# One run of value products per unit: joining a unit's near keys with the last far keys of the unit before

## The chip, the cores and the metric

The kernel runs on one core of a Trainium2 chip. A core has a matrix engine (PE, whose weight loads are shown apart as PEld), a vector engine (DVE), a scalar engine (ACT), a general engine (POOL) and a queue of transfers (SP). PE reads its operands from SBUF and writes to PSUM, eight banks of 2 KB per partition; DVE and ACT copy from PSUM to SBUF. The metric is the device time of one execution in microseconds (us); lower is better.

## The reference

A decoder trunk of two layers over 1024 tokens with 1024 features. Only the attention of the first layer (A) is touched. It has 16 heads in 4 key groups of 4 heads, head width 64, and adds three branches, each with a sigmoid gate of its own:

```python
o = g[..., 0:1] * o_cmp + g[..., 1:2] * o_sel + g[..., 2:3] * o_win
```

`o_cmp` attends to 63 compressed key blocks, `o_win` to a causal window of 256 tokens, and `o_sel` to the 8 selected blocks of 64 keys of each query, out of all keys up to the query. Every branch is a softmax over scores plus a position bias, times values. The kernel computes `o_sel` over all causal keys, with the blocks that are not selected masked in the scores.

## The kernel before

The attention of layer A is worked in 32 *units* (g, t): key group g (4) by tile t (8) of 128 queries, t running fastest. A unit has two kinds of keys. The *near* keys are the window's, 128-key blocks `t-2` to `t` (1 to 3 blocks), together with the compressed blocks (one more block, `pc`). The *far* keys are the blocks 0 to t of the selected branch, t + 1 blocks.

For each kind PE makes scores (`near_scores` L823, `far_scores` L910 and L911, into PSUM bank `s`), DVE adds the bias and takes the minimum (L824, L826, L912), ACT makes exponentials (L803), POOL scales them by gate and denominator (L807). The weights then stand with queries on partitions, and the value products need keys there, so each 128-key block is *turned*: PE transposes it for the four heads into one bank `pt` (L371, 4 instructions; 3 banks), DVE and ACT in turn copy it to an SBUF tile `pT` (L378; 5 tiles), and PE multiplies it by the values (L436): two matmuls per block, one for each half of the heads, whose weights are 64 columns wide and which write partitions 0 to 63 and 64 to 127 of `o`. In the trace each of these matmuls leaves two records, so that a block is four records of L436. The sum of a unit stands in one half of a single PSUM bank `o`, and the two halves are used in turn; DVE copies it out at the end (L925).

`values` (L416) does this for a list of blocks, in *parts* of at most three: the blocks of a part are turned, then multiplied in one chain, the block turned last first. A unit has one near part (up to four products, `pc` the last) and ceil((t + 1) / 3) far parts, so 1, 1, 1, 2, 2, 2, 3, 3 for t = 0 to 7, 15 per group and 60 in all.

`turn(i)` (L959) issues what belongs to turn i: near scores of unit i + 2 (steps a and b), far scores of unit i (f and g), the mask (m), compressed weights (c), far values of unit i - 1 (v) and near values of unit i (n), in the order a m f v b c n g. The framework's scheduler then orders each engine's instructions by its own estimates, within the data dependencies and the orderings that `after(...)` lays down; it pulls transposes and scores in between one another, and does not keep every part's chain in one piece. After the last unit the output projection follows; its weights `ow` are loaded by SP (L1407) as the attention's tiles come free.

Of the kernel before, what the change touches and what calls it, by code (L numbers as in the profile page):

```python
# [129 lines left out]
def trunk(ctx, tc, I, out):  # L130
    nc = tc.nc
# [84 lines left out]
    def after(prev):  # L216
        return tc.issue_after(prev.ins) if prev is not None else ExitStack()
# [38 lines left out]
    def norm_to_hT(p, xget, gains, hH, hL, t0, n, wait=None, behind=(None, None), third=None):  # L256


        xs = []
        for t in range(t0, t0 + n):  # L260
            xt = xget(t)
            xn = p.tile([128, D], F32, name="nxn", bufs=4)
            with after(behind[0]), after(behind[1]):
                rs = row_scale(p, xt, xn, t == 3)
            nc.vector.tensor_scalar(xn, xt, rs, None, op0=OP.mult)
            xs.append(xn)
        for k in range(KC):
            pt = bank("mm")
            for i in range(n):
                mm = nc.tensor.transpose(pt[:, i * 128:(i + 1) * 128], xs[i][:, k * 128:(k + 1) * 128], ident)  # L270
            tk = slice(t0 * 128, (t0 + n) * 128)
            prev = split(hH[k][:, tk], hL[k][:, tk], pt[:, :n * 128], gains[:, k:k + 1])
            turn[0] = mm
            if k == (5 if t0 == 0 else 3) and wait is not None:
                keep(*wait, mm)
            if k == 2 and third is not None:
                third(prev)
        return prev
# [88 lines left out]
    def turned(p, heads, copy, n=128):  # L367

        ps = bank("pt")
        for i, h in enumerate(heads):  # L370
            prev = nc.tensor.transpose(ps[:, i * 128:(i + 1) * 128], h, ident)  # L371
        w = len(heads) * 128
        t = p.tile([128, 512], F32, name="pT", bufs=pt_bufs[0])
        if n < 128:
            copy(t[:, :len(heads) * n].rearrange("p (h q) -> p h q", q=n),
                 ps[:, :w].rearrange("p (h q) -> p h q", q=128)[:, :, 128 - n:])
        else:
            copy(t[:, :w], ps[:, :w])  # L378
        return t, prev
# [8 lines left out]
            self.i += 1  # L388
            return self.parts[(self.i - 1) % len(self.parts)]

    copies, pt_bufs = [0], [5]

    def turn_blocks(p, Ps, vs, late=()):

# [19 lines left out]
                prev = mm  # L414
        return prev

    def values(p, po, Ps, vs, first, last, behind=None, more=None):

        nb = len(vs)
        ends = [nb * (i + 1) // -(-nb // 3) for i in range(-(-nb // 3))]
        for lo, hi in zip([0] + ends, ends):
            ts = []
            for b in range(lo, hi):
                copies[0] += 1
                t, prev = turned(p, [Ps[hp][:, e, b * 128:(b + 1) * 128] for e in range(2) for hp in range(2)],
                                 (nc.scalar.copy, nc.vector.tensor_copy)[copies[0] % 2])
                ts.append(t)
            ops = [(vs[b], vs[b], ts[b - lo][:, :256], ts[b - lo][:, 256:]) for b in reversed(range(lo, hi))]  # L430
            if more is not None and lo == 0:
                ops.append(more)
            for i, (*v, ta, tb) in enumerate(ops):
                with after(prev), after(behind if lo == i == 0 else None):
                    for e, t in enumerate((ta, tb)):
                        mm = nc.tensor.matmul(po[64 * e:64 * e + 64, :256], v[e], t, start=first and lo == i == 0,  # L436
                                              stop=last and hi == nb and i == len(ops) - 1, skip_group_check=True)
                prev = mm
        return prev

    def pipelined(jobs, lag=1):

# [26 lines left out]
    vc = ares.tile([128, G, 128], F32, name="vc")  # L469
# [4 lines left out]
    with ExitStack() as c:  # L474
# [62 lines left out]
        with ExitStack() as c2:  # L537
            np_ = pool(c2, "pn")

            def xget(t):  # L540
                xt = np_.tile([128, D], F32, name="nx", bufs=4)
                nc.sync.dma_start(xt, x_in[t * 128:(t + 1) * 128])
                return xt
# [7 lines left out]
            first = [xget(t) for t in range(2)]  # L551
# [10 lines left out]
            rows_made, behind, rows = None, (None, None), make_rows()  # L562
            for t0 in (0, 2):
                done = t0 * 128, t0 * 128 + 256
                prev = norm_to_hT(np_, lambda t: first[t], g_mix[0], *hT, t0, 2, (fill, 4 if t0 == 0 else 3, ones),
                                  behind, second if t0 == 0 else None)
                behind = prev, scaled_rest[0]
# [12 lines left out]
            prev = norm_to_hT(np_, xlate, g_mix[0], *hT, 4, 4, behind=behind)  # L580
# [58 lines left out]
        steps = compress(0, kc2, wts)  # L639
# [45 lines left out]
        def proj_q(ch):  # L685
            proj_T(wts.load(W[:, 128 * ch:128 * ch + 128], KC, 128), hT, evac_q(ch))
# [3 lines left out]
        steps = compress(1, kc2, wts)  # L690
# [41 lines left out]
        grp = {}  # L732
# [57 lines left out]
        units = [(g, t) for g in range(G) for t in range(NT)]  # L790
# [91 lines left out]
        def near_values(g, t):  # L882
            pc = blocks_[g, t][0]
            pT, _ = turned(wk, [pc[:, 2 * c:2 * c + 2, :] for c in range(2)], nc.vector.tensor_copy)
            po = po_[g, t] = outs()
            k0 = max(t - 2, 0)
            ends[0] = values(wk, po, grp["P2", g, t], [grp["V", 1, g, b // 4][:, b % 4, :] for b in range(k0, t + 1)],
                             True, False, ends[0], (vc[:, g, :64], vc[:, g, 64:], pT[:, :256], pT[:, :256]))

        def far_scores(g, t, hp):  # L890

# [28 lines left out]

        def far_values(g, t):
            po = po_[g, t]
            ends[0] = values(wk, po, grp["P1", g, t], [grp["V", 0, g, b // 4][:, b % 4, :] for b in range(t + 1)],
                             False, True)
            nc.vector.tensor_copy(oT[:, 2 * g:2 * g + 2, tok(t)], po.rearrange("p (c q) -> p c q", q=128))  # L925

        def loads(g, t):
# [22 lines left out]
        for i in (1, 2):  # L950
# [5 lines left out]
        steps = dict(a=lambda u: near_scores(*u, 0), b=lambda u: near_scores(*u, 1), c=lambda u: block_weights(*u),  # L956
                     m=lambda u: block_mask(*u), f=lambda u: far_scores(*u, 0), g=lambda u: far_scores(*u, 1),
                     n=lambda u: near_values(*u), v=lambda u: far_values(*u))
        def turn(i):  # L959
            if 0 <= i < len(units):  # L960
                loads(*units[i])
            if i >= 0:
                load_kw(i + 3)
            for what, d in [('a', 2), ('m', 0), ('f', 0), ('v', -1), ('b', 2), ('c', 2), ('n', 0), ('g', 0)]:
                if 0 <= i + d < len(units):
                    steps[what](units[i + d])
        proj_q(6)
        for i in range(-2, 0):
            turn(i)
# [6 lines left out]
    with ExitStack() as c:  # L976
        kB = pool(c, "aB")
        wk = pool(c, "aw")
# [8 lines left out]
        outs, ends = Turns([o_[:, :256], o_[:, 256:]]), [None]  # L987
# [857 lines left out]
    with ExitStack() as c:  # L1845
        wk = pool(c, "bw")
# [10 lines left out]
        grp = {}  # L1857
# [64 lines left out]
        outs, behind, held, formed = Turns([o_[:, :256], o_[:, 256:]]), [None], [], [None]  # L1922
# [208 lines left out]
```

## Time and profile before

| what | value |
|---|---|
| median of 3 runs | 2744.61 us (2741.62 to 2746.01) |
| the profiled execution | 2744.88 us, of which its span is 2743.1 |
| first and last record of a layer A value product (L436) | starts at 283.0 us and 666.0 us |
| records of L436 on PE | 576 far, 336 near, 128 compressed |
| granted TensorE clock | 0.999 |

The span is what the profiler saw of the program on the core. Where rows are quoted, the busy time of PE is that of pipelined matmuls: the durations of neighbours overlap, and what one costs is read from the start of one to the start of the next. A row of the chain of waits gives the piece of time that the chain spent in a group of instructions, a row of the timeline a start and the time to the last end, with the idle time of PE before it in brackets.

### The profile page before, as it was taken

The numbers are of one execution on the slowest core, as the hardware profiler recorded it, in microseconds if no ns is written. First come the engines' busy times: TensorE is split into PE (matmuls) and PEld (weight loads), VectorE is DVE, ScalarE is ACT, GpSimd is POOL, SyncE is SP. The second block draws the span as 40 slices with busy tenths as digits, with TensorE's granted clock in tenths as the row PEclk, the third lists the DMA queues.
The fourth block names the chain that finished last, engine by engine and source line by source line (L and its number), as shares of the span: only waits on it lengthen the run. The fifth ranks groups of instructions, "written<-read, shape, count | busy, mean of one in ns | idle before, by whom it ended". The sixth has DMA issues, their size and how long they took to land.

```text
span 2743.1 us, 42940 instructions
## 1 busy us (share of the span) xinstructions
PE 2712.7 (99%) x14448; PEld 2211.6 (81%) x14448; DVE 2208.2 (81%) x4532; ACT 1409.4 (51%) x3165; POOL 1385.5 (51%) x1446
## 2 busy tenths in 40 slices
PE   9999999999999999999999999999999999999999
PEld 8988676776888888888878788888878888888887
DVE  5443888987988889899884678688898888898888
ACT  5531776775643343343454444577766443343435
POOL 3135755552365656656446787311104755656562
PEclk9999999999999999999999999999999999999999
DMA  5578663224122222222124455697341211112112
GB/s 174 188 235 299 171 164 104 64 70 146 51 73 66 78 73 67 69 62 77 58 89 125 136 154 165 211 272 235 111 177 50 72 57 58 51 54 62 54 54 77
DMA packets 291900, 312.24 MB, mean 114 GB/s; under 512 B 50300, under 2 KB 229165, under 8 KB 291680
## 3 DMA queue, kind: packets, MB, share of 16 engines
q1 hardware_dynamic: 271280, 247.30, 30.0%
q0 software_dynamic: 20400, 62.20, 7.3%
q8 instruction: 114, 1.87, 0.3%
q14 instruction: 106, 0.87, 0.1%
HBM read 241.99 MB, written 81.04 MB: 118 GB/s over the span
## 4 chain that ended last, share of the span: by engine, by line
PE 86%; DVE 6%; DMA 3%; issue 1%; ACT 1%; POOL 1%; SPq 1%; POOLq 0%; ACTq 0%; DVEq 0%
PE ux L1244 18%; PE uy L1244 15%; PE dx L1054 8%; PE pt L371 6%; PE dr L1054 6%; PE o L436 4%; PE dr L1244 4%; PE mm L239 3%; PE mm L240 3%; PE mm L241 3%; PE o L412 2%; DVE pl L1013 2%; PE s L823 1%; PE dx L1244 1%; PE s L911 1%
## 5 line engine op out<-in xcount | busy, mean ns | idle before, releaser
L1013 DVE TENSOR_TENSOR pl<-oT,ph 128x512 fp32r<-128x512 f32 x336 | 348.7, 1057 | 72.4 <-ACT ph L1012 18.8
L1012 ACT ACTIVATE ph<-oT 128x512 fp32r<-128x512 f32 x342 | 209.7, 627 | 229.9 <-PE ux L1244 54.3
L371 PE MATMUL pt<-ident,P 128*128 128x128 f32 x1536 | 231.5, 277 | 2.9 <-ACT pT L378 1.3
L1013 DVE TENSOR_TENSOR pl<-oTb,ph 128x512 fp32r<-128x512 f32 x228 | 205.7, 926 | 25.1 <-PE dr L1054 17.3
L1012 ACT ACTIVATE ph<-oTb 128x512 fp32r<-128x512 f32 x234 | 142.6, 627 | 159.1 <-PE ux L1244 51.0
L807 POOL TENSOR_SCALAR P<-P,sm,gates 128x384 f32<-128x384 f32 (+7 forms) x256 | 183.1, 726 | 80.2 <-DVE sm L805 57.3
L371 PEld LDWEIGHTS pt<-ident,P 128*128 128x128 f32 x1536 | 174.3, 140 | 59.9 <-issue 42.6
L1449 POOL TENSOR_TENSOR oT<-oT,gffn 128x512 f32<-128x512 f32 x92 | 113.8, 1247 | 214.8 <-DMA oT<-in_ffn_w_up_dram 158.8
L1059 DVE TENSOR_TENSOR xrfx<-xrfx,dr 128x512 f32<-128x512 f32 x320 | 204.1, 679 | 12.9 <-PE dr L1054 12.9
L1059 DVE TENSOR_TENSOR xrfx<-xrfx,dx 128x512 f32<-128x512 f32 x320 | 204.4, 678 | 1.2 <-PE dx L1054 1.2
L1449 POOL TENSOR_TENSOR oTb<-oTb,gffn 128x512 f32<-128x512 f32 x92 | 115.9, 1268 | 151.9 <-DMA oTb<-in_ffn_w_up_dram 85.9
L803 ACT ACTIVATE P<-P,m 128x384 f32<-128x384 f32 (+7 forms) x256 | 170.6, 668 | 35.7 <-DVE m L916 14.1
L378 DVE COPY pT<-pt 128x512 f32<-128x512 f32 (+1 forms) x208 | 131.7, 644 | 34.9 <-PE pt L371 28.3
L1937 ACT ACTIVATE P<-P,st 128x384 f32<-128x384 f32 (+2 forms) x256 | 139.3, 546 | 24.6 <-DVE st L1932 24.3
L378 ACT COPY pT<-pt 128x512 f32<-128x512 f32 x176 | 100.4, 577 | 99.0 <-PE pt L371 98.5
L1932 DVE CUSTOM_DVE_ANT_0 P<-s,T 128x384 f32<-128x384 f32 (+2 forms) x256 | 110.2, 477 | 6.2 <-PE s L1962 1.7
L1054 PE MATMUL dx<-ph,pl 128*128 128x512 f32 x320 | 107.2, 390 | 0.4 <-DVE pl L1013 0.4
L1054 PE MATMUL dx<-ph 128*128 128x512 f32 x320 | 107.3, 389 | 0.0
L912 DVE CUSTOM_DVE_ANT_0 P<-s,T 128x128 f32<-128x128 f32 (+3 forms) x192 | 99.3, 550 | 8.3 <-PE s L911 8.1
L239 PE MATMUL mm<-hH,wh 128*128 128x512 f32 (+1 forms) x272 | 102.8, 379 | 0.0
L240 PE MATMUL mm<-hL,wh 128*128 128x512 f32 (+1 forms) x272 | 102.5, 379 | 0.0
L241 PE MATMUL mm<-hH,wl 128*128 128x512 f32 (+1 forms) x272 | 102.3, 377 | 0.0
(649 smaller groups left out, 8029.1 us busy)
## 6 DMA issues: line engine op xcount, KB each, us to landing
qB<-xrfx POOLq DMA_DIRECT2D x96, 256.0 KB, 5.1
oT<-in_ffn_w_up_dram SPq DMA_DIRECT2D x92, 256.0 KB, 2.9
oTb<-in_ffn_w_up_dram SPq DMA_DIRECT2D x92, 256.0 KB, 2.9
Q<-qB SPq DMA_DIRECT2D x40, 512.0 KB, 7.6
wd<-in_ffn_w_down_dram SPq DMA_DIRECT2D x60, 256.0 KB, 2.6
oT<-in_b_w_q_dram SPq DMA_DIRECT2D x48, 256.0 KB, 3.9
wraw<-in_a_w_in_dram SPq DMA_DIRECT2D x18, 512.0 KB, 5.5
KW<-kS SPq DMA_DIRECT2D x96, 96.0 KB, 2.7
```

Of the source, the lines that this page charges most:

```text
L239: nc.tensor.matmul(ps, lh, rh, start=first, stop=False, skip_group_check=bool(shared))
L240: nc.tensor.matmul(ps, lh, rl, start=False, stop=False, skip_group_check=bool(shared))
L241: return nc.tensor.matmul(ps, ll, rh, start=False, stop=last, skip_group_check=bool(shared))
L371: prev = nc.tensor.transpose(ps[:, i * 128:(i + 1) * 128], h, ident)
L378: copy(t[:, :w], ps[:, :w])
L807: nc.gpsimd.tensor_scalar(P[:, e, :n], P[:, e, :n], sm[:, e:e + 1], gate(e), op0=OP.mult, op1=OP.mult)
L1012: self.high = nc.scalar.activation(h, src, AF.Copy)
L1013: self.last = (eng or nc.vector).tensor_sub(l, src, f32(h))
L1054: nc.tensor.matmul(banks[t], part(a, t)[u], b[v], start=z == 0 and onX != 2, stop=z == 2, skip_group_check=True)
L1059: nc.vector.tensor_add(xs, xs, banks[t])
L1244: mm = nc.tensor.matmul(b, x[:, i * 128:(i + 1) * 128], ys[i], start=first and (z, i) == (0, 0), stop=(z, i) == (2, 3), skip_group_check=True)
L1449: nc.gpsimd.tensor_mul(v, v, gains[:, k:k + 4].unsqueeze(2).to_broadcast([128, 4, 128]))
```

## The change

`values` becomes a generator. With near keys (`first`) it turns the blocks and puts their products on a list `held`, and issues none. With far keys it issues a run of products for each part, and puts what is held behind the last part's products. `value_run` holds the loop that issued the products. In `turn(i)` the step v is split: all far parts of unit i - 1 but the last (`more` of them) are worked where v was, and the last part is turned after n, behind the near blocks of unit i. Its products and the held near products of unit i then go in one run. For the first unit, with no far keys before it, the held products go alone at the end of the turn. `pt_bufs` rises from 5 to 7; before layer B it is set to 6 as before.

```diff
-    copies, pt_bufs = [0], [5]
+    copies, pt_bufs = [0], [7]
...
-    def values(p, po, Ps, vs, first, last, behind=None, more=None):
+    held = []
+
+    def values(p, po, Ps, vs, first, behind, more=None):
...
-            for i, (*v, ta, tb) in enumerate(ops):
-                with after(prev), after(behind if lo == i == 0 else None):
-                    for e, t in enumerate((ta, tb)):
-                        mm = nc.tensor.matmul(po[64 * e:64 * e + 64, :256], v[e], t, start=first and lo == i == 0,
-                                              stop=last and hi == nb and i == len(ops) - 1, skip_group_check=True)
-                prev = mm
-        return prev
+            last = hi == nb and not first
+            ops = [(po, first and i == 0, last and i == len(ops) - 1, op) for i, op in enumerate(ops)]
+            if first:
+                held.extend(ops)
+                continue
+            behind[0] = value_run(ops + (held if last else []), prev, behind[0])
+            if last:
+                held.clear()
+            yield
+
+    def value_run(ops, *prev):
+
+        for dst, starts, stops, (*v, ta, tb) in ops:
+            with ExitStack() as c:
+                for x in prev:
+                    c.enter_context(after(x))
+                for e, t in enumerate((ta, tb)):
+                    mm = nc.tensor.matmul(dst[64 * e:64 * e + 64, :256], v[e], t, start=starts, stop=stops,
+                                          skip_group_check=True)
+            prev = mm,
+        return mm
...
-            ends[0] = values(wk, po, grp["P2", g, t], [grp["V", 1, g, b // 4][:, b % 4, :] for b in range(k0, t + 1)],
-                             True, False, ends[0], (vc[:, g, :64], vc[:, g, 64:], pT[:, :256], pT[:, :256]))
+            for _ in values(wk, po, grp["P2", g, t], [grp["V", 1, g, b // 4][:, b % 4, :] for b in range(k0, t + 1)],
+                            True, None, (vc[:, g, :64], vc[:, g, 64:], pT[:, :256], pT[:, :256])):
+                pass
...
-            ends[0] = values(wk, po, grp["P1", g, t], [grp["V", 0, g, b // 4][:, b % 4, :] for b in range(t + 1)],
-                             False, True)
+            for n, _ in enumerate(values(wk, po, grp["P1", g, t], [grp["V", 0, g, b // 4][:, b % 4, :]
+                                                                   for b in range(t + 1)], False, ends), 1):
+                if n < -(-(t + 1) // 3):
+                    yield
...
-            for what, d in [('a', 2), ('m', 0), ('f', 0), ('v', -1), ('b', 2), ('c', 2), ('n', 0), ('g', 0)]:
+            far = steps['v'](units[i - 1]) if i > 0 else iter(())
+            steps['w'] = lambda u: next(far, None)
+            more = -(-(units[i - 1][1] + 1) // 3) - 1 if i > 0 else 0
+            for what, d in [('a', 2), ('m', 0), ('f', 0)] + more * [('w', -1)] + [('b', 2), ('c', 2), ('n', 0), ('w', -1),
+                                                                                  ('g', 0)]:
                 if 0 <= i + d < len(units):
                     steps[what](units[i + d])
+            if i == 0:
+                value_run(held, None)
+                held.clear()
```

How the scheduler then places the products on PE is shown at two places. In these rows a name is the tile written, then the tiles read; `V` are far values, `VW` near values, `vc` the compressed blocks' values, `P` and `pc` weights that are turned, and the products stand in L436 before and in L452 now. A row with x2 is one block.

The first place is where a group ends and the next begins: the last far part of a group's eighth unit (`V_2907`, three blocks) and the near products of the next group's first unit (`VW_3910` and `vc`). Before, on PE, the far part stood between transposes:

```order
L371 MATMUL pt<-ident,P_3922 128x128
L371 MATMUL pt<-ident,P_4024 128x128
L436 MATMUL o<-pT,V_2907 64x256 x6
L371 MATMUL pt<-ident,P_4376 128x128
L371 MATMUL pt<-ident,P_4509 128x128
```

and the near products came 16 rows later, with that unit's own far block:

```order
L910 MATMUL s<-K_3013,Q_3501 128x256
L911 MATMUL s<-KF_3907,Q_3501 128x256
L436 MATMUL o<-pT,VW_3910 64x256 x2
L436 MATMUL o<-pT,vc 64x256 x2
L436 MATMUL o<-pT,V_3019 64x256 x2
```

Now the two stand in one run:

```order
L927 MATMUL s<-K_3013,Q_3499 128x256
L928 MATMUL s<-KF_3907,Q_3499 128x256
L452 MATMUL o<-pT,V_2907 64x256 x6
L452 MATMUL o<-pT,VW_3910 64x256 x2
L452 MATMUL o<-pT,vc 64x256 x2
L371 MATMUL pt<-ident,P_4123 128x128
L371 MATMUL pt<-ident,P_4206 128x128
```

The second place is the last pair of units on PE, the last far part of the 31st (`V1`) and the near products of the 32nd (`VW10`, `vc`); here the tiles carry their numbers. Before, the near products were a run of their own, ten transposes behind the far run; its head and tail:

```order
L371 MATMUL pt_8642<-ident_67,P23_8283 128x128
L371 MATMUL pt_8683<-ident_67,P1_8533 128x128
L371 MATMUL pt_8690<-ident_67,P1_8533 128x128
L436 MATMUL o_2882<-pT_8647,VW10_7354 64x256 x2
L436 MATMUL o_2882<-pT_8640,VW10_7354 64x256 x2
L436 MATMUL o_2882<-pT_8633,VW10_7354 64x256 x2
L436 MATMUL o_2882<-pT_8626,vc_93 64x256 x2
L371 MATMUL pt_8701<-ident_67,P1_8533 128x128
```

Now seven blocks are multiplied in one run, and the block read first (`pT_8640`) was turned only two transposes ahead of it:

```order
L371 MATMUL pt_8635<-ident_67,P1_8504 128x128
L371 MATMUL pt_8683<-ident_67,P1_8533 128x128
L371 MATMUL pt_8690<-ident_67,P1_8533 128x128
L452 MATMUL o_2882<-pT_8640,V1_7368 64x256 x2
L452 MATMUL o_2882<-pT_8633,V1_7368 64x256 x2
L452 MATMUL o_2882<-pT_8626,V1_7368 64x256 x2
L452 MATMUL o_2882<-pT_8619,VW10_7354 64x256 x2
L452 MATMUL o_2882<-pT_8612,VW10_7354 64x256 x2
L452 MATMUL o_2882<-pT_8605,VW10_7354 64x256 x2
L452 MATMUL o_2882<-pT_8598,vc_93 64x256 x2
L371 MATMUL pt_8683<-ident_67,P1_8657 128x128
```

Over the stage the order has the same 520 value matmuls and 976 transposes on PE, and the same 260 copies of turned blocks, 146 on DVE and 114 on ACT, before and now. The value matmuls stand in 107 uninterrupted runs before and in 72 now; the scores stand in 138 runs before and in 162 now. Ahead of the attention and behind it the order of every engine is the same but for names and line numbers.

## The prediction

> **What bounds the kernel now.** I read the page first, then busy time by stretch, then PE's groups, then PE's timeline. The page:
>
> ```profile
> span 2743.1 us, 42940 instructions
> PE 2712.7 (99%) x14448; PEld 2211.6 (81%) x14448; DVE 2208.2 (81%) x4532; ACT 1409.4 (51%) x3165; POOL 1385.5 (51%) x1446
> PE 86%; DVE 6%; DMA 3%; issue 1%; ACT 1%; POOL 1%; SPq 1%; POOLq 0%; ACTq 0%; DVEq 0%
> ```
>
> PE is busy all the time and holds 86% of the chain of waits, so PE time saved should shorten the span wherever no other engine is close behind. Only the attention of layer A changes. Busy time by stretch (window; PE, PEld, DVE, ACT, POOL; clock, DMA), the second and third key groups cut into units with long scores and the rest, then two 12 us slices:
>
> ```profile
> 384.00:444.00 60.00, 59.20 (x414) 43.02 (x412) 54.90 (x255) 47.00 (x155) 35.79 (x61) 1.00 0.31 90
> 444.00:480.00 36.00, 35.55 (x251) 24.20 (x250) 24.84 (x105) 23.48 (x70) 20.44 (x40) 1.00 0.58 163
> 480.00:540.00 60.00, 59.61 (x418) 43.30 (x419) 55.64 (x261) 46.61 (x151) 34.75 (x60) 1.00 0.22 65
> 540.00:576.00 36.00, 35.06 (x257) 25.49 (x256) 25.43 (x112) 24.54 (x79) 18.82 (x32) 1.00 0.41 112
> 420.00:432.00 12.00, 11.93 (x88) 8.88 (x86) 11.72 (x53) 9.10 (x28) 6.90 (x12) 1.00 0.11 33
> 612.00:624.00 12.00, 11.93 (x86) 8.81 (x86) 11.79 (x53) 9.66 (x29) 6.68 (x10) 1.00 0.00 1
> ```
>
> PE is the bound, with 189.4 of 192 us. But DVE is at 92% in the long stretches (54.90 and 55.64 of 60) and at 98% in single slices. That is where a gain could get lost. The clock is full, so it explains nothing here.
>
> What does PE do there? Its groups between 283 and 667 us (count | busy, mean ns | idle before):
>
> ```profile
> L371 PE MATMUL pt<-ident,P 128*128 128x128 f32 x908 | 137.6, 279 | 2.6 <-ACT pT L378 1.3 <-DVE pT L378 0.9
> L436 PE MATMUL o<-pT,V 128*64 128x256 f32 x576 | 79.0, 392 | 2.4 <-ACT pT L378 1.8 <-DVE pT L378 0.4
> L436 PE MATMUL o<-pT,VW 128*64 128x256 f32 x336 | 43.3, 389 | 2.3 <-ACT pT L378 1.3 <-DVE pT L378 0.7
> L436 PE MATMUL o<-pT,vc 128*64 128x256 f32 x128 | 19.2, 379 | 0.0
> ```
>
> PE waits only 2.4 + 2.3 = 4.7 us for value products' operands, so removing waits can't be worth more. The price must be sought in the runs themselves. The chain of waits cuts PE's time into pieces (start, us, what; x4 of L436 is one block):
>
> ```profile
> 633.24 0.58 PE o L436 x4
> 633.82 0.59 PE pt L371 x4
> 634.40 1.01 PE o L436 x8
> ...
> 637.59 1.45 PE o L436 x12
> ...
> 641.01 1.88 PE o L436 x16
> ...
> 645.98 1.03 PE pt L371 x8
> ...
> 377.24 1.46 PE pt L371 x12
> ```
>
> Four, 8, 12 and 16 product records take 0.58, 1.01, 1.45 and 1.88 us. That is (1.88 - 0.58) / 12 = 0.108 us a record and 0.58 - 4 x 0.108 = 0.15 us once per run, whatever its length. Transposes between two product runs show the same: 0.59, 1.03 and 1.46 us for 4, 8 and 12, so (1.46 - 0.59) / 8 = 0.109 each and 0.15 once. **Each interruption of product runs by transposes thus costs PE 0.15 + 0.15 = 0.30 us that no instruction needs**: a value matmul fills 64 of 128 columns, a transpose all, and going from one to the other and back has a price. Entering from scores costs as much as from transposes:
>
> ```profile
> 648.25 0.40 PE L910 MATMUL s<-K,Q 128*128 128x512 f32 x1
> 648.48 0.39 PE L911 MATMUL s<-K,QM 80*128 80x512 f32 x1
> 648.80 0.65 PE L436 MATMUL o<-pT,V 128*64 128x256 f32 x4
> ```
>
> Scores start 0.23 us apart, the product 0.32 after the last one: 0.09 on entry, the rest of the 0.15 at the way out. Between transposes and scores nothing is paid:
>
> ```profile
> 361.46 1.09 PE L371 MATMUL pt<-ident,P 128*128 128x128 f32 x8
> 362.31 0.48 PE L910 MATMUL s<-K,Q 128*128 128x512 f32 x1
> 362.63 0.39 PE L911 MATMUL s<-K,QM 80*128 80x512 f32 x1
> 362.86 0.40 PE L910 MATMUL s<-K,Q 128*128 128x512 f32 x1
> ```
>
> From 361.46 to 362.63 is 1.17 us: eight transposes at 0.109 (0.87), one score at the 0.23 of the next pair, and 0.07, which is about the 0.15 - 0.09 due for leaving the product run ahead of them.
>
> **The change, part by part.**
>
> *Runs of products.* As issued, 32 near and 60 far runs become 60 and one. The scheduler cuts some: in PE's order 107 uninterrupted runs become 72. I price the order, since PE executes that: 35 x 0.30 = **10.5 us less**. Bounds: if only the 0.15 inside a product run goes away, for the 31 runs that the code joins, 4.6; if all 4.7 us of waits go too, 10.5 + 4.7 = 15.2. I take 10.5, since both halves of the price show at every length of run.
>
> [...]
>
> *Scores in 162 runs for 138.* By the last fence this costs nothing.
>
> *The wait ahead of a joined run.* Its first product reads the block turned last, so it waits for that copy:
>
> ```profile
> L378 DVE COPY pT<-pt 128x512 f32<-128x512 f32 (+1 forms) x144 | 88.5, 627 | 29.5 <-PE pt L371 27.6 <-PE o L436 1.1
> L378 ACT COPY pT<-pt 128x512 f32<-128x512 f32 x114 | 64.9, 577 | 75.0 <-PE pt L371 74.8
> 659.14 1.08 PE L436 MATMUL o<-pT,V 128*64 128x256 f32 x8 [0.62 <-ACT pT L378]
> 664.85 1.52 PE L436 MATMUL o<-pT,V 128*64 128x256 f32 x12 [0.68 <-ACT pT L378]
> ```
>
> A copy takes about 0.6 us, and with nothing between the last transpose and the run PE stands 0.6 to 0.7. Queued behind the run on PE are the unit's far scores (step g), and behind those DVE's bias and minimum and ACT's exponentials. Cover counts, then: pricing the rows between the last transposes that a run needs and the run by the spacings above, 19 of 107 runs have under 0.7 us before, 16 of 72 now. Fewer, but now they are long joined runs. Bounds: in proportion to runs, 4.7 x 72 / 107 = 3.2, 1.5 us gained; if all 16 stand 0.65 and the rest as now, 10.4 against 4.7, 5.7 lost. I take nothing, nearest the 4.7 that 19 such runs cost today.
>
> *Buffers.* A joined run reads up to 3 + 4 = 7 blocks, all seven `pT`, where 5 served runs of four. The next copy waits for the run's end, but its transposes stand behind the run on PE anyway: nothing, at worst one copy's 0.6 us per unit late on an engine that waits for transposes now (27.6 and 74.8 us above). Copies are as many, with the same split.
>
> *The stage's end.* The output projection's loads are issued as the last far scores free their tiles:
>
> ```profile
> 650.42 3.20 SPq L1407 DMA_DIRECT2D ow<-in_a_w_out_dram  x7
> 666.29 0.50 PE L239 MATMUL dx<-ph 128*128 128x512 f32 x1
> ```
>
> From the last far score (648.48, above) to the projection's first matmul PE has 54 transposes and 34 value matmuls in 7 runs before, and 58 and 36 in 6 runs now: 4 x 0.109 + 2 x 2 x 0.108 - 0.30 = 0.6 us more room for the loads, which move with the stage. (A value matmul is two records.) Nothing is lost here.
>
> Sum: 10.5 us of the profiled execution's 2744.88 (span 2743.1, 1.8 outside it), 2734.4; its time is 0.3 above the median of 2744.61, so **2734**.
>
> **The rivals.**
>
> *DVE becomes the bound.* For it: 92% in the long stretches, 98% in slices. Against: DVE's own idle time is mostly waiting for PE (the 27.6 us ahead of copies), which would shrink with PE's. If the long stretches, 60 of 96 us, gained nothing, 36 / 96 x 10.5 = 3.9 us remained: 2740.7. [...]
>
> *Slower: the joined runs stand for their last copy.* 31 times a turn's products now hang on one copy, with the near products, ready long before, behind it. If each stood the full 0.68 us shown above, 21.1 us would be lost against 10.5 gained: 2755. It decides from 10.5 / 31 = 0.34 us per joined run on. Against it: in PE's order most joined runs have transposes or scores between, and before, 19 runs with as little cover cost 4.7 us with all others.
>
> *Nothing changes.* The price belonged to each block and not to the run: against it stand the four lengths above. 2744.6.
>
> **How the numbers follow.** Forecast 0.77, DVE 0.15, slower 0.05, nothing 0.03. The forecast's own range is 2730 (nearly the 15.2) to 2738; the DVE rival pulls the upper end to 2740.5. What a measurement here can tell from no change is about 0.2%, 5.5 us: faster means below 2739.1. Most of the forecast lies there, the DVE rival just outside: faster 0.78, same 0.17, slower 0.05.
>
> **What would show it.** Right: value products on PE in 72 runs with the same 0.108 and 0.15; the stretch from first to last product about 10.5 shorter than its 383; waits ahead of products near 4.7 us. DVE rival: PE idle before scores, released by DVE's minimum, and DVE over 95% in the long stretches. Slower: waits ahead of products over 15 us. It would be wrong, too, if the time moved outside 283 to 667 us, where the order is the same.

## The result, and the profile after

The changed kernel takes **2758.7 us** (median of 6 runs, 2751.3 to 2762.8) against 2744.3 for the kernel before on the same chip: a ratio of **1.0051, with a 95% interval of 1.0037 to 1.0065**. The forecast was 2734 and faster; it is 14 us slower. The profiled execution took 2758.72 us, with a span of 2756.9. The ratio of the kernel with far scores ahead, below, leaves out one execution of 12129.7 us.

The lost time lies where the order changed. These are the first and the last products of the attention in the changed kernel, with PE's view in order of time (start, length, engine, line, operation; in brackets the idle time ahead and what ended it):

```profile
283.19 0.65 PE L452 MATMUL o<-pT,VW 128*64 128x256 f32 x4 [0.45 <-DVE pT L378]
682.16 1.52 PE L452 MATMUL o<-pT,V 128*64 128x256 f32 x12 [0.73 <-ACT pT L378]
683.61 1.19 PE L239 MATMUL dx<-ph 128*128 128x512 f32 x4
```

From the first product to the start of the last record (683.3, the last of the twelve) are 400.1 us; before they were 383.0. That is 17.1 us more, and the span grew by 13.8.

The saving that the forecast counted on is there all the same. PE has 72 runs of products, and a joined run of 28 records looks like this:

```profile
437.36 1.52 PE L452 MATMUL o<-pT,V 128*64 128x256 f32 x12 [0.36 <-DVE pT L378]
438.71 1.47 PE L452 MATMUL o<-pT,VW 128*64 128x256 f32 x12
440.00 0.60 PE L452 MATMUL o<-pT,vc 128*64 128x256 f32 x4
440.54 0.68 PE L927 MATMUL s<-K,Q 128*128 128x384 f32 x2
```

From 437.36 to 440.54 is 3.18 us, and 28 x 0.108 + 0.15 makes 3.17, so the price of a run is what the prediction took it to be. With 35 runs fewer PE's list is 10.5 us shorter, and some 27.6 us came on elsewhere. Two views say where. The first is what PE waited for between the first and last product, before and after (total us, times, longest; the four largest rows of each):

```profile
PE o L436 <- ACT pT L378: 3.1, 6, 0.7
PE pt L371 <- ACT pT L378: 1.3, 3, 0.5
PE o L436 <- DVE pT L378: 1.1, 5, 0.3
PE pt L371 <- DVE pT L378: 1.1, 4, 0.3
```

```profile
PE pt L371 <- POOL P L823: 8.8, 5, 2.7
PE o L452 <- ACT pT L378: 2.7, 7, 0.7
PE s L839 <- DMA KW<-kS: 2.2, 2, 1.1
PE o L452 <- DVE pT L378: 1.9, 6, 0.5
```

The waits ahead of products (PE o), on which the forecast's fear was fixed, are 4.6 us now and were 4.2 by this view. The new ones stand ahead of *transposes*, 8.8 us for POOL's scaling of far weights, where PE waited 0.0 us for POOL before; 2.2 us more are for near keys (`KW`) that come late. All waits of this view add up to 7.3 us before and 21.1 after: 13.8 more.

The second view is a table of stretches (length; busy time of PE, PEld, DVE, ACT and POOL with instructions; PE's granted clock; share of DMA; GB/s):

```profile
451.66:455.07 3.41, 1.29 (x8) 0.67 (x9) 0.72 (x4) 3.39 (x12) 2.41 (x4) 1.00 0.50 159
455.07:458.48 3.41, 3.41 (x20) 1.96 (x18) 0.00 (x0) 0.15 (x1) 1.05 (x2) 0.50 0.00 0
475.55:478.96 3.41, 1.00 (x8) 0.76 (x10) 1.53 (x5) 2.88 (x14) 2.47 (x3) 1.00 1.04 210
478.96:482.37 3.41, 3.41 (x20) 1.92 (x16) 0.20 (x2) 0.00 (x0) 2.91 (x7) 0.50 0.75 238
571.12:574.53 3.41, 1.20 (x9) 0.76 (x7) 2.83 (x19) 3.41 (x14) 0.97 (x2) 1.00 0.98 251
574.53:581.36 6.83, 6.33 (x27) 3.39 (x29) 2.03 (x5) 1.33 (x8) 6.39 (x12) 0.50 0.10 31
```

In 451.66 to 455.07 PE is busy for 1.29 of 3.41 us, and in the next 3.41 us its granted clock is 0.50. The same follows at 478.96 and, for twice as long, at 574.53; there are two more such episodes, at 311.71 and 670.11. Together they are 20.5 us at half clock, so up to 10.2 us lost. Before, the clock was 1.00 throughout these stages.

A wait costs PE more than the idle time in this view, since the records of PE overlap where nothing waits (above, 1.52 us from 437.36 and the next from 438.71). Read from start to start, against the mean spacing of the same two kinds of instruction (transposes, products, scores) without idle time in the kernel before, the 36 places where PE idles cost 13.6 us before, and the 53 now 30.6: 17.0 more. The account is then -10.5 for the runs, +17.0 for waits, up to +10.2 for the clock: 16.7 of the 17.1 us.

What makes POOL late shows at the end of group 1. Ahead is PE, changed kernel:

```profile
475.00 0.28 PE L928 MATMUL s<-KF,Q 128*128 128x256 f32 x1
477.96 0.66 PE L371 MATMUL pt<-ident,P 128*128 128x128 f32 x4 [2.68 <-POOL P L823]
478.54 2.46 PE L452 MATMUL o<-pT,V 128*64 128x256 f32 x12
```

PE stands 2.68 us for the far weights of the group's eighth unit, and then 12 records take 2.46 us that took 1.52 at full clock (above). POOL, changed kernel:

```profile
471.93 0.29 POOL L873 TENSOR_TENSOR pc<-pc,dg 128x60 f32<-128x60 f32 x1 [0.82 <-DVE dg L869]
476.49 0.23 POOL L775 COPY C<-T 128x31 f32<-128x31 f32 x1 [4.27 <-DMA T<-sA]
476.71 2.37 POOL L823 TENSOR_SCALAR P<-P,sm,gates 128x1024 f32<-128x1024 f32 x2
```

and POOL at the same place before:

```profile
463.91 0.29 POOL L857 TENSOR_TENSOR pc<-pc,dg 128x60 f32<-128x60 f32 x1
465.49 2.38 POOL L807 TENSOR_SCALAR P<-P,sm,gates 128x1024 f32<-128x1024 f32 x2 [1.29 <-DVE sm L805]
468.11 0.23 POOL L759 COPY C<-T 128x31 f32<-128x31 f32 x1 [0.24 <-DMA T<-sA]
```

The copy `C<-T` takes 31 columns of the next group's bias out of a tile `T` that a transfer has yet to bring. Before, the scaling (L807) stood ahead of it. Now the copy stands first: POOL waits 4.27 us for the transfer, with the scaling, on which PE waits, queued behind it. PE waits for POOL at five places: 1.74, 2.68 and 2.44 us at the ends of groups 0, 1 and 2, 1.60 at the seventh unit of group 1, and 0.33 near the end. The diff touches neither instruction; the scheduler has placed them anew. Why it chose so, no trace shows.

### The profile page after: what moved, and what is told of

Its sections match the earlier page's. It is cut to its first block, busy times and chain, and to the rows that moved or that the text cites. A ratio compares the mean times of both kernels' runs of the same rounds, so it can differ in the third digit from the quotient of the medians.

```text
span 2756.9 us, 42953 instructions
## 1 busy us (share of the span) xinstructions
PE 2714.7 (98%) x14448; PEld 2218.3 (80%) x14448; DVE 2210.1 (80%) x4532; ACT 1407.8 (51%) x3165; POOL 1382.2 (50%) x1446
## 4 chain that ended last, share of the span: by engine, by line
PE 67%; DVE 4%; DMA 2%; SPq 1%; issue 1%; ACT 1%; POOL 0%; ACTq 0%; POOLq 0%; DVEq 0%
PE ux L1270 19%; PE uy L1270 15%; PE dx L1080 8%; PE dr L1080 6%; PE dr L1270 5%; PE pt L371 2%; PE o L412 2%; DVE pl L1039 1%; PE dx L1270 1%; DMA Q<-qB 1%; PE dx L239 1%; PE dx L240 1%; PE dx L241 1%; PE s L1985 1%; PE s L2002 1%
```

## The experiments

All ratios are to the kernel before, with runs of it on the same chip. "Stretch" is from the first product's start to the last one's in the profiled execution, "waits" the total of PE's waits in it, "half" the time at half clock in it.

| kernel | ratio (95%) | runs on PE | stretch | waits, of them on POOL | half |
|---|---|---|---|---|---|
| before | 1 | 107 | 383.0 | 7.3, 0.0 | 0 |
| changed | 1.0051 (1.0037 to 1.0065) | 72 | 400.1 | 21.1, 8.8 | 20.5 |
| changed, scaling first | 1.0000 (0.9991 to 1.0010) | 72 | 383.4 | 15.7, 1.9 | 0 |
| changed, far scores ahead | 1.0027 (1.0015 to 1.0039) | 74 | 394.6 | 20.1, 7.2 | 6.8 |
| changed, near work ahead | 1.0049 (1.0034 to 1.0064) | 73 | 400.5 | 25.1, 11.2 | 13.7 |
| moved, not joined | 1.0031 (1.0019 to 1.0042) | 99 | 396.9 | 18.9, 4.5 | 10.2 |
| changed, PE kept busy | 1.0029 (1.0018 to 1.0041) | 72 | 389.8 | 15.4, 3.7 | 3.4 |
| before, scaling first | 0.9996 (0.9987 to 1.0005) | 107 | 387.7 | 10.4, 0.0 | 0 |
| scaling first, far scores ahead | 0.9997 (0.9988 to 1.0006) | 74 | 385.1 | 14.2, 3.3 | 3.4 |
| scaling first, KW first | 0.9992 (0.9982 to 1.0001) | 72 | 381.2 | 13.8, 1.9 | 0 |
| these three together | 1.0000 (0.9991 to 1.0009) | 74 | 385.1 | 14.4, 3.3 | 3.4 |
| moved, not joined, scaling first | 1.0007 (0.9998 to 1.0016) | 99 | 388.0 | 15.2, 2.5 | 0 |
| before, seven buffers | 1.0007 (0.9998 to 1.0016) | 107 | 383.2 | 7.4, 0.0 | 0 |
| changed, turning behind the run | 1.0011 (1.0002 to 1.0020) | 70 | 384.2 | 18.0, 0.2 | 0 |
| the same, scaling and KW first | 1.0010 (1.0001 to 1.0019) | 70 | 389.0 | 18.6, 0.0 | 10.2 |
| the same, far scores ahead too | 1.0012 (1.0003 to 1.0021) | 71 | 388.3 | 18.0, 0.0 | 6.8 |

A stretch comes from one execution, and the executions of one kernel lie up to 7.4 us from its median, so small differences between stretches are no verdicts. The kernel before takes 2744.3 us on the first chip and 2746.4 to 2747.8 on those of the experiments, so an expectation in microseconds is compared by its ratio.

The account of the result closes for the other profiles too. For those without half clock in the stretch, the price of the runs and what waits cost from start to start give the change of the stretch to 0.5 us:

| kernel | runs, at 0.30 us each | waits, start to start | sum | stretch, against 383.0 |
|---|---|---|---|---|
| changed, scaling first | -10.5 | 24.0 (+10.4) | -0.1 | +0.4 |
| scaling first, KW first | -10.5 | 22.0 (+8.4) | -2.1 | -1.8 |
| moved, not joined, scaling first | -2.4 | 20.6 (+7.0) | +4.6 | +5.0 |
| changed, turning behind the run | -11.1 | 25.9 (+12.3) | +1.2 | +1.2 |
| before, scaling first | 0 | 18.1 (+4.5) | +4.5 | +4.7 |
| before, seven buffers | 0 | 13.9 (+0.3) | +0.3 | +0.2 |

**1. POOL's order alone.** The bias copies are ordered behind the latest scaling:

```diff
-                    nc.gpsimd.tensor_copy(C[:, hh, :31], every[:, 1:])
+                    with after(scaled[0]):
+                        nc.gpsimd.tensor_copy(C[:, hh, :31], every[:, 1:])
...
-                nc.gpsimd.tensor_scalar(P[:, e, :n], ...)
+                scaled[0] = nc.gpsimd.tensor_scalar(P[:, e, :n], ...)
```

> The changed kernel with one difference: POOL makes its copies of the next bias (line 775 of the changed kernel) behind the latest scaling of far weights instead of ahead of it. PE's order stays, with 72 runs of products. Queue theory (the stretch is longer because a group's last scaling stands on POOL behind a copy that waits for a load, and because TensorE's clock is halved after the gap that this makes): the gaps that PE has at 477.96 (2.68 us) and 575.03 (2.44 us) go, with the three episodes of half clock behind them (3.41 and 6.83 us at half, 5.1 us lost): 10 us less than the changed kernel's 2758.7, so about 2748. Place theory (the far scores stand on PE behind the last far part and the joined run, so that minimum, exponentials, scaling and turning of a unit all come later, whatever POOL's order is): the gaps become smaller by the load's wait alone and others grow, 2755 to 2759. Joining theory (joined runs stand for their last copy): no change, 2758.

Measured 1.0000, 0.5% less than the changed kernel, with PE's products in the same 72 runs (from here on, the mended kernel). The order of DVE, of ACT and of SP's transfers is that of the changed kernel, and so is PE's but for the four transposes of one block near the end of the stage; on POOL only these copies have moved, at the ends of groups 0, 1 and 2. POOL at the end of group 1, in this kernel:

```profile
468.90 2.38 POOL L824 TENSOR_SCALAR P<-P,sm,gates 128x1024 f32<-128x1024 f32 x2 [1.24 <-DVE cm L843]
471.23 0.56 POOL L776 COPY C<-T 128x31 f32<-128x31 f32 x3
472.25 0.23 POOL L776 COPY C<-T 128x31 f32<-128x31 f32 x1 [0.46 <-DMA T<-sA]
```

The scaling stands ahead of the copies, PE's waits for POOL fall from 8.8 to 1.9 us (the three at the groups' ends are gone, the 1.6 us of the seventh unit stays), and in the profiled execution the clock stays at 1.00 through the attention. The queue theory holds for the whole loss against the kernel before. But no more: 10.5 us of saving are still missing. PE's waits in this kernel (the five largest rows):

```profile
PE o L452 <- ACT pT L378: 2.9, 8, 0.7
PE o L452 <- DVE pT L378: 2.7, 7, 0.8
PE s L840 <- DMA KW<-kS: 2.7, 2, 2.1
PE pt L371 <- POOL P L824: 1.9, 2, 1.6
PE s L928 <- DVE cm L843: 0.9, 4, 0.3
```

The profiled execution, 2744.05 us, lies 3.3 us under the median of this kernel's ten. Over the ten the granted clock averages 0.9983, over the 18 of the kernel before on that chip 0.9992. From that I estimate 2.5 us (0.0009 of 2744) for the clock in a usual execution of this kernel, which the profile doesn't show.

**2. The far scores, or the near work, ahead.** Two other orders of a turn's steps:

```diff
-... more * [('w', -1)] + [('b', 2), ('c', 2), ('n', 0), ('w', -1), ('g', 0)]:
+... more * [('w', -1)] + [('b', 2), ('c', 2), ('g', 0), ('n', 0), ('w', -1)]:   (far scores ahead)
+... more * [('w', -1)] + [('n', 0), ('w', -1), ('b', 2), ('c', 2), ('g', 0)]:   (near work ahead)
```

> The changed kernel with its turn's steps in another order: the far scores of the unit (g) are issued ahead of the near weights' turning (n) and of the last far part with the joined run (w). The runs are joined as before, 74 of them on PE. Place theory: the chain from far scores to turned far weights starts earlier by the length of the near turning and joined run, the gaps of 1.6 to 2.7 us at the transposes of the last units go and the clock stays up, so the 10 us that the joining saves come through: 2734 to 2740. Queue theory: the bias copies still stand ahead of the scaling and their load still waits for the last unit's far scores, which come earlier too: part of it, 2742 to 2752. Joining theory: the joined run stands for its last copy here as well, with less behind it to cover: 2758 or more.

> The changed kernel with its turn's steps in another order: near turning and joined run (n, w) directly behind the other far parts, and the steps b, c (near scores of later units) behind them, the far scores g last as in the changed kernel. 73 runs on PE. Place theory, with far scores no earlier against the turn's end: no gain or little, 2752 to 2758; if what is late is the near work's place rather than that of the far scores, 2738 to 2745. Queue theory: POOL's copies stand as they did, 2755 to 2759. Joining theory: more joined runs without cover, since nothing lies between the last turning and the run: above 2760.

The far scores ahead gave 1.0027: about half of the loss, in the range of the queue theory, for the copy still stands ahead of the scaling (PE waits 3.28 us there). PE's waits for POOL fell only from 8.8 to 7.2 us, so most of the gain goes with the shorter time at half clock, 6.8 for 20.5 us. The near work ahead gave nothing, 1.0049.

**3. Moved, not joined.** The held near products are issued as a run of their own, behind the unit's last far scores:

```diff
-            behind[0] = value_run(ops + (held if last else []), prev, behind[0])
-            if last:
-                held.clear()
+            behind[0] = value_run(ops, prev, behind[0])
...
-                    nc.tensor.matmul(ps[:, :max(rw, 256)], ql[:nr], kl[:nr, ks], start=False, stop=True)
+                    far_last[0] = nc.tensor.matmul(ps[:, :max(rw, 256)], ql[:nr], kl[:nr, ks], start=False, stop=True)
...
-            if i == 0:
-                value_run(held, None)
+            if held:
+                ends[0] = value_run(held, ends[0], far_last[0])
```

> The changed kernel with the far part moved as it is, but the held near products not joined to it: they are issued as a run of their own behind the unit's last far scores. 99 runs of products instead of 72, at 0.30 us a run 8 us more for PE. Place and queue theories: the late chain stays and the saving of the joining goes, partly covered by PE's gaps: 2760 to 2768. Joining theory: the stall for the last copy and the lateness go with the joining, 2745 to 2752.

1.0031 lies between the two expectations, and its interval reaches into that of the joining theory, so the time alone does not rule it out. The waits do: ahead of products there are 5.7 us here and 4.6 in the joined kernel, so the joining brought no stall for its last copy. PE still waits 4.5 us on POOL, half as long as in the joined kernel, so the moving alone makes POOL late. That the kernel came out no slower than the joined one, with 27 runs more, goes with this and with its shorter time at half clock, 10.2 for 20.5 us.

**4. PE kept busy.** 14 more transposes, with overwritten results, ahead of four far turnings that wait:

```diff
+        for i in range(fill):
+            nc.tensor.transpose(ps[:, :128], heads[0], ident)
         for i, h in enumerate(heads):
             prev = nc.tensor.transpose(ps[:, i * 128:(i + 1) * 128], h, ident)
```

> The changed kernel with 14 more transposes (1.5 us of PE, their result is overwritten) ahead of the first far transposes of the four units at which PE stands 1.6 to 2.7 us for POOL (the eighth of groups 0, 1 and 2, the seventh of group 1). Nothing becomes ready sooner. Clock theory (PE idle over some 60% of a 3.41 us window gives half the clock in the next window): the half-clock episodes at 455, 479 and 574 us go or become fewer, 3.4 to 6.8 us less, the extra transposes lie in the gaps and cost at most 2 us: 2751 to 2756. Rival (the clock falls for another reason, or the time at half clock lies beside other waits and costs nothing): 2758 to 2765, the same or worse by what doesn't fit the gaps.

With 56 transposes more, 6.1 us of work at 0.109 each, the kernel is *faster* than the changed one, 1.0029 for 1.0051, though the two intervals overlap a little (1.0037 to 1.0041). The table of stretches in this kernel:

```profile
444.00:468.00 24.00, 23.42 (x165) 17.49 (x161) 16.65 (x70) 14.98 (x45) 12.39 (x22) 1.00 0.47 137
468.00:492.00 24.00, 21.48 (x158) 15.48 (x157) 14.15 (x65) 14.69 (x56) 12.45 (x25) 0.93 0.53 132
564.00:588.00 24.00, 23.24 (x184) 17.95 (x183) 16.42 (x80) 16.75 (x61) 12.50 (x25) 1.00 0.38 100
```

The changed kernel shows 0.93, 0.93 and 0.86 there. At the first and the last place the filling has kept the clock up; at the second a wait of 2.39 us is left, and the clock of the stretch is 0.93. Not all of the gain is the filling's: the episodes at 311 and 670 us, where nothing was added, are gone too. And the profiled execution, 2751.3 us, lies 2.8 us under this kernel's median, at a granted clock of 0.999 where its six executions average 0.9983, so its time at half clock is probably less than usual.

**5. Is POOL's order a gain by itself?** The edit of experiment 1, made to the kernel before:

> The kernel before with POOL's bias copies behind the latest scaling, as it was done to the changed kernel; 107 runs of products as before. Queue theory (the harm came about only because the change moved a scaling behind a copy that waits): nothing to gain here, where POOL idles 11.3 us for those copies but PE waits only 0 to 1 us for POOL: 2743 to 2747. Rival (the new POOL order is a gain of its own for any kernel, so that the joining with it brings nothing by itself): 2735 to 2740.

0.9996: no. It mends what the change broke and nothing else.

**6. What is still missing.** Two edits on top of the scaling first: the far scores ahead (as in 2), or near keys loaded ahead of a turn's other loads:

```diff
-            if 0 <= i < len(units):
-                loads(*units[i])
             if i >= 0:
                 load_kw(i + 3)
+            if 0 <= i < len(units):
+                loads(*units[i])
```

> Both edits that had an effect of their own together: the far scores of a unit issued ahead of its near turning and joined run, and POOL's bias copies behind the latest scaling of far weights. Theory as it stands now (the joining saves 10 us of PE, and lost them again since the last scaling of a group stood on POOL behind a copy that waits for a load, and since the clock was halved after that; what is left over is the late chain of scores, exponentials and scaling): the scaling first gave 13 us over the changed kernel, the far scores ahead gave 5; what the second gives beside the first is that part of its 5 which lies in gaps that the first leaves (1.6 us at 451 and some 4 us of small ones), so 2742 to 2746. Rival (the two edits remove one and the same lateness): as the scaling first alone, 2747. Rival (they add in full): 2741 or below, which would beat the kernel before.

> The changed kernel with the scaling first, and with the loads of near keys (KW) issued ahead of a turn's other loads. In the kernel with the scaling first PE waits 2.7 us for KW at 307 to 311 us, where SP issues them 3 us later than before, behind bias loads. Theory (part of what the scaling first doesn't give back is SP's queue in the first group): 2 to 3 us less than 2747.3, so 2744 to 2745.5. Rival (the first group's start is bound by other waits, DVE's minima above all, and the late load only takes their place): 2747.

0.9997 and 0.9992, neither clearly below 1. The first is nearest the rival that both edits take away the same lateness, but its interval reaches into the theory's range as well. The second removed the waits for KW (2.7 us in experiment 1); the 2.2 us that it gained are about what was expected, and less than the uncertainty of 3.6. It has the lowest ratio of the study, with an interval that just reaches 1. All three edits together:

> The changed kernel with three edits: POOL's bias copies behind the latest scaling, a turn's near keys loaded first, and the far scores ahead of the near turning and joined run (without the edit that put the far transposes behind the products). Theory (each takes away waits of its own: 13 us, 2.4 us and 1 us of the profiled spans so far): a ratio to before of 0.9985 to 0.9990, the best of the study, and the first clearly below 1. Rival (what is left is bound by the chain from scores to scaling and by DVE, so that a wait taken away comes back elsewhere): 0.9990 to 0.9999.

1.0000, nearest the rival: PE's waits are 14.4 us, where they are 13.8 without the far scores ahead.

**7. Turning behind the run.** At 451 us in experiment 1 PE stands 1.6 us at a block's transposes for POOL, with a joined run of 28 records behind them. So the far transposes of a unit were ordered behind the last products of the unit before:

```diff
-                t, prev = turned(p, [...], ...)
+                with after(None if first or lo else behind[0]):
+                    t, prev = turned(p, [...], ...)
```

> The changed kernel, with its own order on POOL and its own loads, and the far transposes of a unit behind the last products of the unit before. Theory (POOL's order is the main cause): the 1.6 us at 454 go, and with them the half clock behind; the gaps of 2.4 to 2.7 us at the eighth units stay, as nothing else is ready there: 3 us less, a ratio to before of 1.0035 to 1.0045. Rival (PE's order is the main cause, and POOL's would have cost nothing with another): 1.0000 to 1.0010.

> The changed kernel with the scaling first, the near keys' loads first, and one more: the far transposes of a unit are issued behind the last products of the unit before, so that no transposes that wait for POOL's scaling stand on PE ahead of a joined run that is ready. In the profiles so far that happens at one unit (the seventh of group 1: 1.6 us ahead of a run of 28 records), while in group 2 the run goes first and nothing is waited for. Theory (these 1.6 us and the 0.9 us like it at 652 are waits in the wrong place): 1.5 to 2.5 us below the kernel without it, a ratio to before of 0.9983 to 0.9987. Rival (the chain from scores to scaling is late by as much and the wait comes behind the run): 0.9990 to 0.9995 as without it.

> The same with the far scores ahead of the near turning and joined run as well. Theory (the scaling chain has its longest cover here, and nothing waits for it): all of the joining's 10 us less the waits of the first group, ratio 0.9970 to 0.9980. Rival (beside the other edits this one gives nothing, as it gave 1 us beside the scaling first alone): 0.9980 to 0.9992.

For the mended kernels this is a loss (1.0010 and 1.0012 against 0.9992 and 1.0000; the second is within the uncertainty): the wait was no accident of PE's order, it only moved behind the transposes, to the run, 2.86 us at that place in the first of them. On the changed kernel it gave 1.0011, against my expectation of 1.0035 to 1.0045. The reason shows on POOL at the end of group 1:

```profile
467.88 2.38 POOL L824 TENSOR_SCALAR P<-P,sm,gates 128x1024 f32<-128x1024 f32 x2 [1.60 <-DVE sm L822]
470.36 0.23 POOL L776 COPY C<-T 128x31 f32<-128x31 f32 x1
```

An edit to PE's order made the scheduler put the scaling ahead of the copy again, with no edit to POOL. The waits on POOL fell to 0.2 us, but those ahead of products rose from 4.6 to 11.9; the gain goes with the clock, which stayed up in the profiled execution (2745.0 us, 5.0 under this kernel's median). Since both orders changed here, it is experiment 1 that speaks against the rival. Over the whole study this order divides the moved kernels: the five with the copy ahead of the scaling at the end of group 1 lose 0.27 to 0.51%, the eight with the scaling ahead, reached in two ways, at most 0.12%.

**8. Does a run's price count in time?** The mended kernel without the joining, and the buffers by themselves (`pt_bufs` 7 in the kernel before):

> The far part moved as in the changed kernel and POOL's scaling first, but the near products not joined: a run of their own behind the unit's far scores, 99 runs of products for 72. If the runs' price is paid in time, 27 x 0.30 = 8.1 us more than the mended joined kernel (ratio 1.0000): 1.0030, and the stretch from first to last product 8 us longer than its 383. If waits for the chain of scores and scaling and for DVE take up what the joining saves: 1.0000 to 1.0010, with 3 to 8 us fewer waits on PE than the joined one has.

> The kernel before with seven buffers for turned weights in place of five, nothing else. As put in the forecast: nothing, 0.9993 to 1.0007. Rival (the later release of buffers holds back the copies, and seven are a gain of their own): 0.9980 to 0.9990. Rival (with more buffers the turning runs ahead of other work on DVE and ACT and makes the scaling late): 1.0010 to 1.0030.

Unjoined: 1.0007 against 1.0000 joined, 1.9 us. With 2.5 us of uncertainty on each, that is -1.6 to 5.4 us, below the 8.1 that 27 runs cost on PE's list. The stretches, 388.0 and 383.4, say 4.6. The table of accounts splits that: 8.1 us saved by the joining, and 3.5 lost again to dearer waits (24.0 for 20.6 us, by start to start; by idle time they are nearly the same, 15.7 and 15.2). In time no share can be given, from nothing to two thirds of the price. Seven buffers: 1.0007, an interval that holds 1, and the same waits: no effect that can be measured.

## Why the prediction was wrong

*What bounds the kernel* and *Runs of products* stood: PE's list sets the end, a run costs 0.15 + 0.15 us, 35 runs went, and PE's list became 10.5 us shorter; with it the account closes in six more profiles. *Scores in 162 runs for 138* and *Buffers* held too.

**The step that failed is "The wait ahead of a joined run".** It named the right things ("queued behind the run on PE are the unit's far scores, and behind those DVE's bias and minimum and ACT's exponentials"), and then asked only for the wait ahead of products, which stayed at 4.6 us, within its bounds, and set the term to nothing. It did not ask who waits for those exponentials in the end: POOL's scaling, and behind it PE itself at the next transposes. In the changed kernel that is 8.8 us of new waits. With POOL's order mended PE still idles 8.4 us more than before (15.7 for 7.3): 2.7 for near keys, 2.5 more for DVE's minima ahead of scores, 1.9 for POOL, 1.4 more ahead of products. From start to start that is 10.4 us, all of the saving. Two thirds of it, 7.0, are there without the joining too, so they belong to the moving.

**Two things had no step at all.** POOL's queue: the far weights share it with copies that wait for transfers, and the order in which two such instructions stand is the scheduler's choice. Experiment 1 puts its price, with the clock's, at 0.5%. And the clock: the sum took a wait to cost its own length. In the changed kernel the waits of 1.60 and 2.68 us were each followed by 3.41 us at half clock, up to 1.7 us more, and that of 2.44 us by 6.83, up to 3.4 more; the one of 1.74 us was followed by full clock. The reading that removing waits can't be worth more than 4.7 us went by idle time as well; from start to start all of PE's waits in the stretch cost 13.6 before.

Of the rivals, *nothing changes* is nearest to what the joining is worth when mended, but for another reason: the price does belong to the run. *Slower: the joined runs stand for their last copy* gave 2755, close to 2758.7, and is wrong nevertheless: it wanted over 15 us of waits ahead of products. *DVE becomes the bound* is not what happened to the changed kernel. In the mended one PE's waits for DVE's minima ahead of scores are 3.2 us where they were 0.7 before, a part of what it foretold; but DVE is busy for 54.8 and 56.2 of 60 us in the long stretches there, under the 95% that it wanted.

What is left open: which of the small waits of the mended kernel could be taken away, and why the moving brings them. In the later groups it does save, measured at the copies of the units' results: from the last unit of group 1 to that of group 2 it takes 93.4 us, 95.3 before, and group 3 takes 87.9 for 90.2. The first two groups end 5.0 us later, of which a part is only that a unit's last far part now stands behind the next unit's near blocks: at the last far score of group 1 the kernel is 2.7 us late. The edits tried there moved the waits rather than took them away.

## What to carry to other kernels

The price of moving a piece of work later on a busy engine is more than the wait at its own place: follow what comes behind it through every engine back to the first, and read on each queue which instruction that waits for a transfer stands next to the chain. Where a scheduler orders the queues, compare the order on the engines that the change does *not* touch, at the ends of groups above all, where loads for the next group are consumed. And allow for more than its idle time in the price of a wait of PE: here some 0.15 us at each (13.6 us for the 36 of 8.5 us idle before), and behind three of the changed kernel's four waits of 1.60 to 2.68 us time at half clock, up to 1.7 us lost behind two of them and up to 3.4 behind the third.

## What the runs showed of the hardware

In the profiled execution of the changed kernel the clock goes to half in steps of 3.41 us that lie on one raster: the episodes begin at 311.71, 455.07, 478.96, 574.53 and 670.11 us, 42, 7, 28 and 28 steps apart, and last one step each, the fourth two. Each begins at the end of a step in which PE was busy for little of the 3.41 us: 1.50, 1.29 (a pause of 1.60 us and smaller ones), 1.00, 1.20 and 2.01 us. The longest pauses that reach into these five steps are 1.13, 1.60, 2.68, 2.44 and 0.91 us, so none was as long as a step. The emptiest of the other full-clock steps in that attention, from 373.15 us, was busy for 1.90 us and was followed by full clock, and so were all with more than 2.01. In the kernel that was moved and not joined, a step of 1.63 us was followed by half clock and one of 1.59 by full clock, and nothing here shows what decided. By its table of stretches:

```profile
459.11:462.52 3.41, 1.63 (x13) 0.98 (x15) 0.33 (x2) 3.19 (x12) 2.53 (x3) 1.00 0.51 157
462.52:465.93 3.41, 3.41 (x15) 2.37 (x12) 1.82 (x5) 0.59 (x1) 0.71 (x2) 0.50 0.00 2
667.33:670.74 3.41, 1.59 (x13) 0.92 (x14) 0.19 (x2) 1.77 (x5) 1.74 (x2) 1.00 0.89 228
670.74:674.15 3.41, 3.41 (x32) 2.43 (x33) 1.69 (x3) 0.59 (x1) 0.64 (x1) 1.00 0.94 338
```

In the changed kernel, then, half clock went with how little PE was busy in a whole step, more than with the length of one pause. A pause of 1.60 us was followed by half clock (at 454.03, in the step with 1.29 us busy), one of 1.74 us by full clock (at 374.66, in the step with 1.90). In experiment 1 one of 1.59 us was followed by full clock (at 451.14, in 3.41 us with 1.62 busy).
